# Forgetting attention with its scores made twice, in a hybrid trunk on one core

## The chip, the cores and the metric

The kernel runs on one core of a Trainium2 chip. The metric is the device time of one execution in microseconds. A core has five engines with queues of their own that work strictly in order: PE (matrix multiplication, with its weight loads PEld beside it), DVE (vector), ACT (scalar functions), POOL (the general vector engine) and SP, which here issues every DMA. Matmuls write PSUM, eight banks of 128 partitions by 512 floats; the other operands lie in SBUF. POOL reads and writes SBUF here, DVE and ACT both memories.

## The reference

One layer on x (2048 x 1024): h = RMSNorm(x); a projection of h to about 8,200 columns feeds three branches and a set of gates. The branches are forgetting attention (8 heads of 64), a gated delta rule (4 heads of 128 behind a causal convolution of four taps) and attention on a memory of 256 rows. Each branch is multiplied by a SiLU gate, projected to 1024 channels, weighted by a sigmoid gate and added; an output projection, the residual and a last RMSNorm follow. The part that matters here:

```python
s = jnp.einsum('bqhd,bkhd->bhqk', q_blk, k) * scale          # scale = 1/8
s = s + F_blk[..., :, None] - F[:, :, None, :]               # F: running sum of log-sigmoid
s = jnp.where(pos[None, None, None, :] <= p_blk[None, None, :, None], s, -jnp.inf)
p = jax.nn.softmax(s, axis=-1)
return jnp.einsum('bhqk,bkhd->bqhd', p.astype(v.dtype), v)   # then * silu(az)
```

All of it is float32. The kernel splits an operand into a high part of the matmul's rounded format (`F32R`) and a low part, the rest, and adds the products that matter.

## The kernel before, in words

A small planner (`Plan`) writes the program. Parts of the work are generators that say when their next step could start and how long it takes on PE; the planner keeps a clock for PE, ACT, DVE, POOL and the DMA queue, with costs by line, and always issues the first part that is ready, the dense matmuls last. The order that it finds is the order of the program on every engine; nothing is decided at run time.

The dense work, `dense()`, runs through the whole kernel: the input projection (tiles `pd_in`, 128 channels by 512 rows in 24 matmuls), then the branch projections (`branch`, tiles `pbr`, 12 matmuls each, for branch 1, branch 2, and the first two groups of 512 rows of branch 0, which is attention), then `branch_half` (tiles `pba`) for the other two groups, woven with the output projection (`pout`). The side work fills in: norm, logits, memory attention, the delta rule in three parts, and last `part_fox`, the forgetting attention. `part_fox` starts when the first half of the gate projections is done; from there the dense work beside it is the second half of the gate projections, then `pbr`. A `pbr` of branch 0 for a group of rows needs the attention output of all heads for that group (`load_ya`), so of the last head too.

In `part_fox` a unit is one head and 256 queries, 64 units in all, and three generators share the work. `prep` loads K and V of a head and splits them. `scores` makes, for each block of 128 queries, the scores with queries on the partitions: for each chunk of up to 512 keys two matmuls into a bank (L1084, L1087), the terms of F carried by four more rows of the operands, on the last chunk a third, of bfloat16, that adds the causal mask (L1086); DVE copies the bank to the tile `pr` and takes its maximum in the same instruction (L1088). `exps` gives ACT the exponential with the maximum as bias and the sum as a second output (L1106), and sends the reciprocals of the sums to DRAM. `values` transposes the probabilities on PE, four blocks of 128x128 to a bank (L1176, tile `ptp`); ACT rounds the bank to `ph` (L1181) and DVE subtracts, bank minus `ph`, to `plo` (L1182); two tiles later PE multiplies both with V (L1162, L1164, into `po`). `finish` loads the SiLU gate (`za`) and the reciprocals (`zl`), POOL multiplies the output with both, and SP stores it.

## Time and profile before

| what | number |
|---|---|
| median of 3 runs | 2749.91 us (2745.09 to 2751.78) |
| the profiled execution | 2749.7 us |
| its span, first to last instruction | 2747.7 us |
| mean granted clock of PE | 0.986 |
| PE, PEld | 96%, 80% of the span |
| DVE, ACT, POOL | 47%, 43%, 24% |
| bytes read and written | 213.75 and 133.40 MB |

A row of a group of instructions gives the line, the engine, the operation, what it writes and reads with the shapes and the count, then busy time and the mean time of one in ns, then the idle time of the engine before them and what ended it. Rows of a tile give count, shortest, median and longest time in ns, and the first and last start in us. Rows in order of time give the start and the time of one in us. Matmuls overlap, so their own times add up to more than PE's; the distance from one start to the next is what one costs.

### The profile page before, as it was taken

To read this page: it belongs to the slowest core of one execution; us is meant where nothing else is said; L and a number is where in the kernel's file an instruction comes from. 1 tells how busy PE (TensorE), PEld (TensorE's weight loads), DVE (VectorE), ACT (ScalarE), POOL (GpSimd) and SP (SyncE) were. 2 spreads that over 40 slices of the span, in tenths; PEclk is the share of its full clock that TensorE was granted. 3 is DMA by queue.
4 is the path that set the end of the run, shared out by engine and by line. 5 is a ranking of instruction groups with operands and counts; after the bars stand their busy time and mean duration, and the time that the engine had idled before them with its cause. 6 is when DMAs were issued, how large, how long until landed. Compare 5 with 4: busy or idle time off the path is not lost. (4 is left out here: it accounts for less than half of the span.)

```text
span 2747.7 us, 39152 instructions
## 1 busy us (share of the span) xinstructions
PE 2644.6 (96%) x13896; PEld 2196.4 (80%) x13896; DVE 1295.6 (47%) x3119; ACT 1182.4 (43%) x2469; POOL 657.5 (24%) x551
## 2 busy tenths in 40 slices
PE   7999999999999999899999999999999989988998
PEld 6778888888888888688788778788888778767887
DVE  6442656665333338122221356556556756334444
ACT  5531224342674421144334475666666645112221
POOL 0101110011333321222221432333333311453200
PEclk9999999999999999999999999999999999999999
DMA  5122222222656542455453332322222554888433
GB/s 184 51 79 84 85 84 66 70 85 77 202 184 205 187 147 85 135 161 157 151 159 121 102 81 65 78 69 76 85 75 60 136 144 117 295 279 287 152 122 108
DMA packets 256115, 349.74 MB, mean 127 GB/s; under 512 B 57808, under 2 KB 152272, under 8 KB 255648
## 3 DMA queue, kind: packets, MB, share of 16 engines
q1 hardware_dynamic: 255920, 347.25, 40.7%
q8 instruction: 109, 1.79, 0.3%
q14 instruction: 86, 0.70, 0.1%
HBM read 213.75 MB, written 133.40 MB: 126 GB/s over the span
## 5 line engine op out<-in xcount | busy, mean ns | idle before, releaser
L362 PE MATMUL pd_in<-hh,wh_in 128*128 128x512 f32 x1984 | 803.9, 405 | 8.5 <-ACT evg L399 8.5
L364 PE MATMUL pd_in<-hh,wl_in 128*128 128x512 f32 x1984 | 784.4, 395 | 3.5 <-POOL wl_in L346 2.4
L363 PE MATMUL pd_in<-hl,wh_in 128*128 128x512 f32 x1984 | 784.2, 395 | 0.0
L364 PEld LDWEIGHTS pd_in<-hh,wl_in 128*128 128x128 f32 x1984 | 374.4, 189 | 92.8 <-POOL wl_in L346 7.7
L362 PEld LDWEIGHTS pd_in<-hh,wh_in 128*128 128x128 f32 x1984 | 375.4, 189 | 83.6 <-ACT evg L399 8.9
L363 PEld LDWEIGHTS pd_in<-hl,wh_in 128*128 128x128 f32 x1984 | 375.4, 189 | 73.4
L346 POOL TENSOR_TENSOR wl_in<-wr_in,wh_in 128x1024 fp32r<-128x1024 f32 x88 | 214.6, 2440 | 908.9 <-ACT wh_in L342 860.2
L1182 DVE TENSOR_TENSOR plo<-ptp,ph 128x512 fp32r<-128x512 f32 (+1 forms) x288 | 178.6, 656 | 107.5 <-ACT ph L1181 106.5
L1106 ACT ACTIVATE pr<-pr,mx 128x1024 f32<-128x1024 f32 (+2 forms) x192 | 172.9, 902 | 93.6 <-DVE mx L1096 93.0
L1088 DVE TENSOR_SCALAR_CACHE_REDUCE pr<-pss 128x512 f32<-128x512 f32 (+2 forms) x320 | 185.7, 602 | 51.7 <-PE pss L1087 50.2
L1181 ACT CAST ph<-ptp 128x512 fp32r<-128x512 f32 (+1 forms) x288 | 149.6, 566 | 62.4 <-PE ptp L1176 61.1
L1162 PE MATMUL po<-ph,Vs 128*128 128x256 f32 x576 | 148.3, 294 | 17.7 <-ACT ph L1181 17.7
L342 ACT CAST wh_in<-wr_in 128x1024 fp32r<-128x1024 f32 x88 | 92.2, 1048 | 155.3 <-PE pd_in L363 147.5
L1176 PE MATMUL ptp<-ident,pr 128*128 128x128 f32 x1088 | 150.8, 274 | 4.2 <-ACT pr L1106 4.2
L1361 PE MATMUL pbr<-yh,wbh 128*128 128x512 f32 x320 | 129.1, 403 | 18.8 <-DVE gt L1386 9.9
L1176 PEld LDWEIGHTS ptp<-ident,pr 128*128 128x128 f32 x1088 | 126.4, 141 | 13.2 <-ACT pr L1106 4.9
L1164 PE MATMUL po<-plo,Vs 128*128 128x256 f32 (+1 forms) x512 | 133.4, 289 | 3.0 <-DVE plo L1182 2.5
L1162 PEld LDWEIGHTS po<-ph,Vs 128*128 128x128 f32 x576 | 110.2, 192 | 29.4 <-ACT ph L1181 21.2
L1362 PE MATMUL pbr<-yl,wbh 128*128 128x512 f32 x320 | 127.3, 398 | 1.9 <-DVE yl L558 1.9
L1363 PE MATMUL pbr<-yh,wbl 128*128 128x512 f32 x320 | 126.5, 395 | 0.0
L1087 PE MATMUL pss<-K,Q 128*128 128x512 f32 (+2 forms) x320 | 125.8, 396 | 0.5 <-POOL K L1008 0.5
L1084 PE MATMUL pss<-K,Q 128*128 128x512 f32 (+2 forms) x320 | 122.0, 382 | 1.5 <-DVE pr L1088 1.3
(324 smaller groups left out, 4410.6 us busy)
## 6 DMA issues: line engine op xcount, KB each, us to landing
wr_in<-in_w_in SPq DMA_DIRECT2D x88, 512.0 KB
dgt<-evg SPq DMA_DIRECT2D x96, 256.0 KB
gt<-dgt SPq DMA_DIRECT2D x96, 256.0 KB
dpt<-gt SPq DMA_DIRECT2D x80, 256.0 KB
pp<-dpt SPq DMA_DIRECT2D x64, 256.0 KB
dgq<-evv SPq DMA_DIRECT2D x48, 256.0 KB
kqv<-dgq SPq DMA_DIRECT2D x16, 768.0 KB
xt<-in_x SPq DMA_DIRECT2D x16, 512.0 KB
```

The source lines that it names most:

```text
L346: nc.gpsimd.tensor_sub(lo, raw, hi.bitcast(F32))
L362: nc.tensor.matmul(ps, wh[:, k, :], xh[:, k, :], start=(k == 0), stop=False)
L363: nc.tensor.matmul(ps, wh[:, k, :], xl[:, k, :], start=False, stop=False)
L364: nc.tensor.matmul(ps, wl[:, k, :], xh[:, k, :], start=False, stop=(k == kt - 1))
L1088: nc.vector.tensor_scalar(pr[:, ks], ps[:, 0:w], 1.0, None, ALU.mult, ALU.max, accum_out=nmx[:, j, ck:ck + 1])
L1106: nc.scalar.activation(pr[:, es], pr[:, es], AF.Exp, bias=mx[:, j:j + 1], scale=0.125, accum_out=lsp[:, j, e:e + 1])
L1162: nc.tensor.matmul(dst, Vk, ph[:, src], start=(v == 0 and b == 0), stop=False)
L1164: nc.tensor.matmul(dst, Vk, plo[:, src], start=False, stop=False)
L1176: nc.tensor.transpose(pt[:, o0:o0 + P], prs[j][0][:, (2 * v + b) * P:(2 * v + b + 1) * P], ident)
L1181: nc.scalar.copy(ph[:, 0:w], pt[:, 0:w])
L1182: nc.vector.tensor_sub(plo[:, 0:w], pt[:, 0:w], ph[:, 0:w].bitcast(F32))
L1361: nc.tensor.matmul(ps, wh[:, k, :], yh, start=(k == 0), stop=False)
```

## The change

Attention now works on units of one head and 512 queries, 32 in all. The scores are made twice.

`maxima` makes them with queries on the partitions, from the high parts alone (one matmul over 68 rows, tile `psm`), and only takes their maxima: DVE reduces each bank, the diagonal block after a mask add. The four maxima per partition are split in a high and a low part, transposed by one matmul (`ptm`) and written into eight more rows of the query operand `QA`, one pair for each block of 128 queries, so that the second scores come out with the maximum subtracted.

`values` makes the scores again with keys on the partitions (two matmuls, tile `pst`, up to 512 queries each), so that no transposes are needed: the mask is added by DVE in PSUM on diagonal blocks, ACT takes the exponential into `p` in SBUF, ACT rounds `p` to `ph`, DVE subtracts `p` minus `ph` to `plo`, and PE multiplies both with V over 512 queries. The sums over keys now run across partitions: POOL adds each `p` to a running tile `acc`, and `sums` splits it on DVE, sums it over the partitions with a matrix of ones on PE (`pL`), sends the row through DRAM to come back as 128x4, takes reciprocals there, and sends these through DRAM for the product. The bank rings are now two for maxima, two for scores, one for outputs and one for everything else.

The buffer of the convolution's input grows from 515 to 544 columns; the columns that are used stay the same.

```diff
-    dL = [dram.tile([256], F32, name=f"dL{n}") for n in range(8 * (S // 256))]
+    dL = [dram.tile([512], F32, name=f"dL{n}") for n in range(8 * NG)]
+    dR = [dram.tile([512], F32, name=f"dR{n}") for n in range(8 * NG)]
...
-            xb = hpA.tile([P, 515], F32, tag="xb", name="xb", bufs=2)
+            xb = hpA.tile([P, 544], F32, tag="xb", name="xb", bufs=2)
...
-        rs, rp, ro = Ring(psx, "s", 2), Ring(psx, "p", 3), Ring(psx, "o", 1)
+        rs, rp, ro, rm = Ring(psx, "s", 2), Ring(psx, "p", 2), Ring(psx, "o", 1), Ring(psx, "m", 1)
...
+                for ck in range(G + 1):
+                    for j in range(4):
+                        ks = slice(ck * 512, ck * 512 + (512 if ck < G else (j + 1) * P))
                         w = ks.stop - ks.start
...
-                        nc.tensor.matmul(ps[:, 0:w], Q1h[:, qs], K1h[:, ks], start=True, stop=False)
-                        if ck == nck - 1:
-                            nc.tensor.matmul(ps[:, w - P:w], identb, mneg, start=False, stop=False)
-                        nc.tensor.matmul(ps[:, 0:w], Q2h[:, qs], K2h[:, ks], start=False, stop=True)
-                        nc.vector.tensor_scalar(pr[:, ks], ps[:, 0:w], 1.0, None, ALU.mult, ALU.max,
-                                                accum_out=nmx[:, j, ck:ck + 1])
...
+                        nc.tensor.matmul(ps[:, 0:w], QAn[0:68, j * P:(j + 1) * P], KAh[0:68, ks], start=True, stop=True)
+                        e = pl.pe + pl.LAT
+                        if ck == G:
+                            nc.vector.tensor_tensor(dg[:, j, :], ps[:, w - P:w], mneg, ALU.add)
+                            e = pl.dve(P, e)
+                            w -= P
+                        if w:
+                            nc.vector.tensor_reduce(nmx[:, j, ck:ck + 1], ps[:, 0:w], AX.X, ALU.max)
...
+                nc.tensor.transpose(pt[0:104, 0:P], mt.bitcast(F32), ident)
+                nc.vector.tensor_tensor(QAn[96:104].rearrange("p (j n) -> p j n", j=4),
+                                        pt[96:104, 0:P].unsqueeze(1).to_broadcast([8, 4, P]), blk[96:104], ALU.mult)
...
+        def sums(n, oT, acc, ta):
...
+            nc.vector.tensor_copy(ah, acc)
+            nc.vector.tensor_sub(al, acc, ah.bitcast(F32))
...
+            nc.tensor.matmul(pL, ones, ah, start=True, stop=False)
+            nc.tensor.matmul(pL, ones, al, start=False, stop=True)
...
+            nc.scalar.copy(Ls, pL[0:1])
...
+            t1 = move(dL[n], Ls, 2)
...
+            t1 = move(lr, dL[n].rearrange("(p j) -> p j", j=4), 2)
...
+            nc.vector.reciprocal(rl, lr)
...
+            t1 = move(dR[n].rearrange("(p j) -> p j", j=4), rl, 2)
...
-                                nc.tensor.transpose(pt[:, o0:o0 + P],
-                                                    prs[j][0][:, (2 * v + b) * P:(2 * v + b + 1) * P], ident)
...
-                        nc.scalar.copy(ph[:, 0:w], pt[:, 0:w])
-                        nc.vector.tensor_sub(plo[:, 0:w], pt[:, 0:w], ph[:, 0:w].bitcast(F32))
...
+                        nc.tensor.matmul(ps[:, 0:w], KAh[:, ks], QAn[:, c0:512], start=True, stop=False)
+                        nc.tensor.matmul(ps[:, 0:w], KBh[:, ks], QBn[:, c0:512], start=False, stop=True)
+                        p = fx.tile([P, 512], F32, tag="p", name="p", bufs=3)
+                        t1 = pl.pe + pl.LAT
+                        if t >= 4 * G:
+                            nc.vector.tensor_tensor(ps[:, 0:P], ps[:, 0:P], mnegT, ALU.add)
+                            t1 = pl.dve(P, t1)
+                        nc.scalar.activation(p[:, 0:w], ps[:, 0:w], AF.Exp, scale=0.125)
...
+                        nc.scalar.copy(ph[:, 0:w], p[:, 0:w])
+                        t2 = pl.act(w, t1)
+                        nc.vector.tensor_sub(plo[:, 0:w], p[:, 0:w], ph[:, 0:w].bitcast(F32))
+                        t2 = pl.dve(w, t2)
+                        if t:
+                            nc.gpsimd.tensor_add(acc[:, c0:512], acc[:, c0:512], p[:, 0:w])
+                            ta = pl.pool(w, max(ta, t1))
```

The change also moves work on every engine. The first place is PE where attention ends. Before, the last value matmuls (`po`) are followed by branch projections (`pbr`) of branch 2, group 2:

```order
L1162 MATMUL po<-ph,Vs 128x128
L1164 MATMUL po<-plo,Vs 128x128
L1192 MATMUL po<-plo,Vs 128x256
L1361 MATMUL pbr_2_21930<-yh,wbh_20358 128x512
L1362 MATMUL pbr_2_21930<-yl,wbh_20358 128x512
L1363 MATMUL pbr_2_21930<-yh,wbl_20360 128x512
```

In the changed kernel the last projection of branch 2 (group 3) stands ten units of attention before the end:

```order
L1389 MATMUL pbr_3_19679<-yh,wbh_18095 128x512
L1390 MATMUL pbr_3_19679<-yl,wbh_18095 128x512
L1391 MATMUL pbr_3_19679<-yh,wbl_18097 128x512
L1216 MATMUL po<-ph,Vs 128x512
L1218 MATMUL po<-plo,Vs 128x512
L1183 MATMUL pst<-QA_12109,KA_12105 128x256
L1184 MATMUL pst<-QB_12111,KB_12107 128x256
```

and its last value matmuls stand among the projections of branch 0, with the first `pba` 24 `pbr` and two `pL` matmuls behind them:

```order
L1216 MATMUL po<-ph,Vs 128x128
L1218 MATMUL po<-plo,Vs 128x128
L1219 MATMUL po<-plo,Vs 128x512
L1389 MATMUL pbr_1_22378<-yh,wbh_19903 128x512
L1390 MATMUL pbr_1_22378<-yl,wbh_19903 128x512
L1391 MATMUL pbr_1_22378<-yh,wbl_19905 128x512
```

So the branch projections that stood behind attention now stand beside it, and in between lie eight units with hardly any of them.

The second place is POOL in the second half of attention. Before, it splits queries and weights and multiplies outputs:

```order
L346 TENSOR_TENSOR wl_in_2_17117<-wr_in_2_17028,wh_in_2_17115 128x1024
L1130 TENSOR_TENSOR oT<-oT,za 64x256
L1053 TENSOR_TENSOR Q_1_12116<-qr,Q_1_12116 64x256
L1131 TENSOR_TENSOR oT<-oT,zl 64x256
L1130 TENSOR_TENSOR oT<-oT,za 64x256
```

In the changed kernel, in a unit without filler:

```order
L1200 TENSOR_TENSOR acc<-acc,p 128x512 x8
L1200 TENSOR_TENSOR acc<-acc,p 128x384
L1200 TENSOR_TENSOR acc<-acc,p 128x256
L1061 TENSOR_TENSOR QB_12110<-qr,QA_12108 64x512
L1200 TENSOR_TENSOR acc<-acc,p 128x128
L1152 TENSOR_TENSOR oT<-oT,zl 64x512
L1151 TENSOR_TENSOR oT<-oT,za 64x512
```

An addition to `acc` for each tile of probabilities has come in, between the products with loaded tiles that were there.

The third place is DVE, at the end of a unit. Before, it copies scores, takes maxima and subtracts from PSUM (`ptp`):

```order
L1182 TENSOR_TENSOR plo<-ptp,ph 128x512 x2
L1182 TENSOR_TENSOR plo<-ptp,ph 128x384
L1088 TENSOR_SCALAR pr,nmx<-pss 128x512 x2
L1095 TENSOR_REDUCE mx<-nmx 128x1
L1096 TENSOR_SCALAR mx<-mx 128x1
```

In the changed kernel:

```order
L1197 TENSOR_TENSOR plo<-p,ph 128x384
L1188 TENSOR_TENSOR pst<-pst,mnegT 128x128
L1197 TENSOR_TENSOR plo<-p,ph 128x256
L1087 TENSOR_TENSOR dg<-psm,mneg 128x128 x2
L1119 CAST ah<-acc 128x512
L1197 TENSOR_TENSOR plo<-p,ph 128x128
L1120 TENSOR_TENSOR al<-acc,ah 128x512
```

The subtraction now reads `p` from SBUF, and the mask adds and the split of the sum have come in between.

More of the change, by code (lines that the diff above doesn't have):

```diff
@@ L959, in part_fox @@
         psx = fs.enter_context(tc.tile_pool(name="psx", bufs=2, space=PSUM))
-        rs, rp, ro = Ring(psx, "s", 2), Ring(psx, "p", 3), Ring(psx, "o", 1)
+        rs, rp, ro, rm = Ring(psx, "s", 2), Ring(psx, "p", 2), Ring(psx, "o", 1), Ring(psx, "m", 1)
         LAG = 2
-        XW = 1024
         fx = fs.enter_context(tc.tile_pool(name="fx", bufs=1))
-        mneg = fx.tile([P, P], BF16, name="mneg")
-        identb = fx.tile([P, P], BF16, name="identb")
+        KA = [fx.tile([P, S], F32R, name=f"KA{i}") for i in range(2)]
@@ L966, in part_fox @@
+        KB = [fx.tile([P, S], F32R, name=f"KB{i}") for i in range(2)]
+        QA = [fx.tile([P, 512], F32R, name=f"QA{i}") for i in range(2)]
+        QB = [fx.tile([P, 512], F32R, name=f"QB{i}") for i in range(2)]
+        blk = fx.tile([P, 4, P], F32, name="blk")
+        ones = fx.tile([P, P], F32R, name="ones")
+        mneg = fx.tile([P, P], F32, name="mneg")
         nc.gpsimd.memset(mneg, 0.0)
         nc.gpsimd.affine_select(mneg, mneg, [[-1, P]], ALU.is_ge, -1e30, base=0, channel_multiplier=1)
-        nc.vector.tensor_copy(identb, ident)
@@ new lines, in part_fox @@
+            eng.memset(KA[i][96:104].bitcast(F32), -1.0)
+        nc.vector.memset(ones.bitcast(F32), 1.0)
+        nc.gpsimd.memset(blk, 1.0)
+        nc.gpsimd.affine_select(blk, blk, [[-2, 4], [0, P]], ALU.is_ge, 0.0, base=-96, channel_multiplier=1)
+        nc.gpsimd.affine_select(blk, blk, [[2, 4], [0, P]], ALU.is_ge, 0.0, base=97, channel_multiplier=-1)
+        mts = [fx.tile([P, 104], F32R, name=f"mt{i}") for i in range(2)]
+        for i in range(2):
+            nc.vector.memset(mts[i].bitcast(F32), 0.0)
@@ L1017, in prep @@
                         nxt = raw(dv[g + 1], "vr")
-                    yield later(t0, rs.when), 0.44
-                    pt, kb = rs.take("ptv")
+                    yield later(t0, rm.when), 0.44
+                    pt, kb = rm.take("ptv")
                     pt = four(pt)
@@ L1195, in values @@
                 nc.scalar.activation(oT, po[64:128], AF.Copy, scale=0.5)
                 nc.vector.scalar_tensor_tensor(oT, po[0:64], 0.5, oT, ALU.mult, ALU.add)
-                ro.done(ko, pl.dve(256, pl.act(256, pl.pe + pl.LAT)))
-                finish(n, oT, r, hp, g, us)
+                ro.done(ko, pl.dve(512, pl.act(512, pl.pe + pl.LAT)))
                 st["pv"] = n + 1
+                pl.add(sums(n, oT, acc, ta))
+        OB = 3
         pl.add(values())
-        pl.add(scores())
+        pl.add(maxima())
```

275 lines of the change are left out of this document (128 added, 147 removed).

## Prediction

> **What bounds the kernel now.** I read the page's busy row first, then where the attention stage begins and ends, then its windows.
>
> ```profile
> span 2747.7 us, 39152 instructions
> PE 2644.6 (96%) x13896; PEld 2196.4 (80%) x13896; DVE 1295.6 (47%) x3119; ACT 1182.4 (43%) x2469; POOL 657.5 (24%) x551
> L1084 PE MATMUL pss<-K,Q x320: 218/393/628, 1537.8 to 2308.1; 128*128 128x512 f32 x128, 128*128 128x128 f32 x16, 128*128 128x384 f32 x16
> L1162 PE MATMUL po<-ph,Vs x576: 220/280/583, 1556.4 to 2327.1; 128*128 128x256 f32 x192
> L1487 PE MATMUL pba<-yh,wbh x128: 277/283/415, 2509.3 to 2608.8; 128*128 128x256 f32 x128
> 1537.80:2330.00 792.20, 763.33 (x4556) 647.95 (x4556) 474.30 (x1515) 502.10 (x1050) 246.30 (x254) 0.98 0.34 89
> 2330.00:2509.30 179.30, 158.84 (x668) 126.25 (x667) 58.36 (x80) 26.60 (x42) 79.71 (x63) 0.97 0.86 284
> ```
>
> PE is 96% busy, so PE sets the time. The window rows give length, then busy PE, PEld, DVE, ACT, POOL, the granted clock, the DMA share and GB/s. Attention runs from 1537.8 (first `pss`) to about 2327 (last `po`), woven with dense matmuls; after it PE still has 179 us of branch projections (`pbr`) before the first `pba` at 2509.3. Everything that the change touches lies between 1537.8 and 2509.3, 971.5 us, and the rest to the end is 2747.7 - 2509.3 = 238.4 us. Inside, DVE is busy 474 of 792 us and POOL 246: both have room today.
>
> A busy time of PE counts overlapping matmuls, so I price PE by start-to-start times:
>
> ```profile
> 2100.10 0.28 PE L1162 MATMUL po<-ph,Vs 128*128 128x256 f32 x1
> 2100.22 0.28 PE L1164 MATMUL po<-plo,Vs 128*128 128x256 f32 x1
> 2101.01 0.40 PE L1087 MATMUL pss<-K,Q 128*128 128x512 f32 x1
> 2101.24 0.40 PE L1084 MATMUL pss<-K,Q 128*128 128x512 f32 x1
> 2101.48 0.23 PE L1086 MATMUL pss<-mneg,identb 128*128 128x128 bf16 x1
> 2101.51 0.48 PE L1087 MATMUL pss<-K,Q 128*128 128x512 f32 x1
> 2101.83 0.28 PE L1162 MATMUL po<-ph,Vs 128*128 128x256 f32 x1
> 2110.49 1.47 PE L1176 MATMUL ptp<-ident,pr 128*128 128x128 f32 x12
> 2111.71 0.48 PE L362 MATMUL pd_in<-hh,wh_in 128*128 128x512 f32 x1
> ```
>
> So 512 columns cost 0.23 us, 256 cost 0.12, a transpose 1.22/12 = 0.10, a mask matmul 0.12 (0.03 until the next starts, which then takes 0.32, not 0.23). For 384 columns I put 0.175, between the two.
>
> **The change, part by part, on PE.** Removed: 1088 transposes (111 us at 1.22/12), 128 masks (15), 640 score matmuls (448 of 512 columns, 64 each of 384, 256 and 128: 103 + 25 = 128), and the value matmuls, 1024 of 256 and 128 of 128 columns (136): 390 us. Added: 320 score matmuls for the maxima (224 of 512, 32 each of 384, 256, 128: 51.5 + 12.6 = 64), 640 transposed score matmuls (128), 640 value matmuls over 512 queries (128), 64 of 512 against a matrix of ones for the sums (15), 32 transposes of the maxima (3): 338-339 us. The 128 transposes of V (11) stay. **PE saves 51 us.** If PE stayed the bound throughout, that would be the gain.
>
> The instruction order speaks against that. The dense filler beside attention is 1126 `pd_in` and 960 `pbr` matmuls before (259 + 221 = 480 us); the changed order issues 35 of the first before attention starts, which then starts 8 us later, at 1546. In 1546 to the first `pba` it has three parts:
> - A: 22 of the 32 attention units (212 of 320 key tiles), with 1091 `pd_in` and 768 `pbr`. PE: 212/320 of 350 us = 232, plus 251 and 177, 660 us.
> - B: 8 units (80 tiles) with only 18 `pbr`: 87 + 4 = 91 us of PE. No filler is left; the first group of branch 0, which comes next, needs the last head.
> - C: the last two units (28 tiles) with 174 `pbr`: 31 + 40 = 71 us.
>
> Before, all this filler outlasted attention; now attention outlasts it, and part B goes at the pace of the slowest other engine.
>
> **The pace of attention without filler.** Durations:
>
> ```profile
> L1182 DVE TENSOR_TENSOR plo<-ptp,ph 128x512 fp32r<-128x512 f32 x224 | 145.4, 686 | 99.2 <-ACT ph L1181 98.3
> L1182 DVE TENSOR_TENSOR plo<-ptp,ph 128x384 fp32r<-128x384 f32 x64 | 35.3, 552 | 8.3 <-ACT ph L1181 8.2
> L1196 DVE SCALAR_TENSOR_TENSOR oT<-po,oT 64x256 f32<-64x256 f32 x64 | 26.6, 416 | 46.2 <-ACT oT L1195 43.3 <-DMA dL<-rl 2.1 <-DMA qr<-dq 0.2
> L1390 POOL TENSOR_TENSOR gt<-gt,pp 128x512 f32<-128x512 f32 x46 | 59.3, 1297 | 62.9 <-DVE gt L1386 51.9 <-DMA pp<-dpt 10.8
> L1008 POOL TENSOR_TENSOR K<-kr,K 64x512 fp32r<-64x512 f32 x32 | 40.8, 1280 | 58.3 <-ACT K L1004 54.3 <-DMA zl<-dL 3.9
> L1053 POOL TENSOR_TENSOR Q<-qr,Q 64x256 fp32r<-64x256 f32 x62 | 45.6, 736 | 196.6 <-ACT Q L1046 145.8 <-issue 25.8 <-DMA wr_in<-in_w_in 10.0
> L399 ACT ACTIVATE evg<-pd_in,bmg 128x512 f32<-128x512 f32 x48 | 33.0, 688 | 14.6 <-PE pd_in L364 13.9 <-ACT K L1006 0.2
> L557 ACT CAST yh<-yr 128x512 fp32r<-128x512 f32 x42 | 25.8, 620 | 107.1 <-DMA yr<-dym 54.5 <-DMA yr<-dya 22.2 <-DMA yr<-dyb 17.2
> ```
>
> One head has 40 tiles: 28 of 512 queries, 4 each of 384, 256, 128.
> - POOL (its old work was light; the running sum `acc` is new): 24 adds of 512 at 1.30, 12 narrow ones at 1.02, 0.74, 0.45 (by line between 1297 and 736) = 40; K, Q and the two products on the output, 16 of 64x512 at 1.28 = 20. 60 us.
> - DVE: 28 `plo` at 0.69 and 12 narrow (0.55, 0.42, 0.28) = 24; 24 maxima over 512 at 0.69 and 12 narrow = 22 (no such reduction is in the rows; the nearest row of 512 from PSUM is 686); 32 mask adds of 128 at 0.28 = 9; copies and splits of the sum 7; some 2.8 per unit for small steps = 11; V 2. 74 us.
> - ACT: exp 28 at 0.69, cast 28 at 0.62, narrow ones 10, K and Q copies 10, output and sums 6: 63 us.
> - PE: 44 us.
>
> By busy time alone DVE sets 74 us a head, 148 us in B (two heads' worth of tiles). That is the floor of B; the other end comes from what DVE and POOL do to each other.
>
> ```profile
> L1182 DVE TENSOR_TENSOR plo<-ptp,ph x288: 536/681/693, 1551.9 to 2325.2; 128x512 fp32r<-128x512 f32 x112, 128x384 fp32r<-128x384 f32 x32
> L558 DVE TENSOR_TENSOR yl<-yr,yh x48: 676/691/1594, 2167.8 to 2537.8; 128x512 fp32r<-128x512 f32 x48
> L418 DVE TENSOR_SCALAR evv<-xb,cw x48: 486/489/2248, 264.7 to 694.3; 128x512 f32<-128x512 f32 x48
> 2362.63 1.29 POOL L1390 TENSOR_TENSOR gt<-gt,pp 128x512 f32<-128x512 f32 x1 [3.02 <-DVE gt L1386]
> 2362.87 1.59 DVE L558 TENSOR_TENSOR yl<-yr,yh 128x512 fp32r<-128x512 f32 x1 [0.32 <-ACT yh L557]
> 281.57 2.40 POOL L346 TENSOR_TENSOR wl_in<-wr_in,wh_in 128x1024 fp32r<-128x1024 f32 x1 [22.95 <-ACT wh_in L342]
> 282.01 2.25 DVE L418 TENSOR_SCALAR evv<-xb,cw 128x512 f32<-128x512 f32 x1 [3.17 <-ACT xb L415]
> ```
>
> The three numbers are min, median, max in ns. `plo` today subtracts an SBUF tile from a PSUM tile, and never takes over 693 ns. `yl` is the same subtraction with both inputs in SBUF: 0.69 us alone, up to 1.59; the one at 2362.87 ends 0.54 us after the POOL add that was running, as if it had waited for it. So does the single-source `evv` at 282.01. **The new `plo` has both inputs in SBUF (`p`, `ph`), and the new `acc` add runs on POOL once for nearly every tile.** If they take turns, a head needs POOL's 60 us plus DVE's own operations of this kind (24 `plo` and 7): 91 us, with the rest of DVE hidden under POOL's turns. B is then 183 us. I take this end, since the rows show it wherever the two meet.
>
> [...]
>
> C by the same turns: 28 tiles at 91/40 = 2.28 us is 64, plus 16 additions to `gt` at 1.30 (21) and 12 `yl` at 0.69 (8): 93 us, over PE's 71. A by the same turns: 212 x 2.28 = 483, 23 weight splits `wl_in` at 2.40 (55), 24 `wbl` of 128x512 (31), 32 `gt` (42), 32 `yl` (22): 633 us, under PE's 660. So A stays with PE, and I give it the loss that the stage has today: PE work before is 401 + 480 = 881 of 971.5 us, 10.3% over (waits, and a clock of 0.98). 660 x 1.103 = 728 us.
>
> The conv buffer (544 columns, not 515) changes no instruction's size: `evv` reads the same 512 columns. It costs nothing while PE is the bound there; at worst (the 144 + 48 conv instructions a tenth slower, uncovered) 14 us, at best a few us gained. The two loads and stores more per unit for the sums (a row out, back as 128x4, the reciprocal out) hang only on the output, three buffers deep, and SP issues fewer DMAs in all (8 for each of 32 units, before 6 for each of 64); uncovered only behind the last unit, where 24 `pbr` and 96 `pba` matmuls (5 + 12 us) stand ahead of the first that need it. I put 0, at worst 12 us.
>
> **Sum:** 1545.8 + 728 + 183 + 93 + 238.4 = 2788 us of span; the profiled execution took 2749.7 for a span of 2747.7, so 2 us lie around it: 2790 us. The profiled execution is within 0.2 us of the median of the three runs, 2749.91.
>
> **Rivals.**
> 1. *DVE and POOL hardly collide.* For: POOL's adds may fall into DVE's PSUM reads, whose durations never stretch. Against: `yl`. B takes DVE's 148, C PE's 71 x 1.103 = 78: 2738 span, 2740 us.
> 2. *PE's saving arrives.* DVE's small work overlaps better than in-order queues suggest, and B runs near PE's 91 x 1.1 = 100 with C 78: 2690 span, 2692 us. Against: 74 us of DVE work a head.
> 3. *The turns bite in A too.* [...] DVE also empties the score banks, two per ring; a late `plo` delays the next maximum, and then PE. POOL's products with the loaded reciprocals stand ahead of `acc` adds in its queue. If this doubles the loss in A, it adds 68 us, and the late output 12: 2868 span, 2870 us. It decides from the point where a wait of 1.3 us per tile no longer fits the two tiles between exp and value matmul.
>
> **How the numbers follow.** Forecast 0.52, rival 1 0.17, rival 2 0.07, rival 3 0.24. A change under 0.3% (8 us) can't be told from none here. The forecast's own range is 2755 to 2825 (A's loss between 7 and 14%, B between 170 and 195 us); all but its lowest edge is slower. Rival 1 at 2740 is at the edge of faster, so I split it: faster 0.09 + 0.07 = 0.16, the same 0.08 and 0.02 of the forecast = 0.10, slower 0.74. The range runs from below rival 1 to rival 3: 2725 to 2870. I predict **2790 us, 1.5% slower.**
>
> **What would show it.** In the changed profile: new `plo` with a mean clearly over 0.69 us and a maximum near 2 (right), or at 0.69 (rival 1); a stretch without `pd_in` and `pbr` of some 183 us in which PE is busy about half and POOL plus `plo` fill the time; PE's idle time put down to ACT and DVE tiles of attention, where before it had little; the last `po` within some 15 us of the first `pba`, not 182; the part before 1546 and the last 238 us unchanged. The prediction is wrong if that stretch is shorter than 150 us, or if A loses much more than a tenth.

## The result: 4.1% slower, and the profile after

| | before | changed |
|---|---|---|
| median | 2750.66 us (4 runs on the same chip) | 2861.10 us (4 runs, 2856.40 to 2867.26) |
| ratio | 1 | 1.0407, 95% interval 1.0382 to 1.0432 |
| profiled execution, its span | 2749.7, 2747.7 us | 2867.26, 2865.2 us |

The forecast was 2790 us, 1.5% slower, with a range of 2725 to 2870. The direction was right and the time lies in the range, but the loss is 110 us where 40 were forecast. First the head of the page of the changed kernel.

```profile
span 2865.2 us, 36512 instructions
...
PE 2686.9 (94%) x12584; PEld 2157.1 (75%) x12584; DVE 1618.1 (56%) x2896; ACT 1177.3 (41%) x2373; POOL 1036.0 (36%) x751
...
PE   7999999999999998999999999998988887788998
...
PEclk9999999999999999999999999999989976779999
```

PE is less busy than before (94% instead of 96%), DVE and POOL much more (DVE 1618 us instead of 1296, POOL 1036 instead of 658). In the last fifth of the span PE falls to 8 and 7 tenths, and the clock that was granted to it to 7 and 6. The rows of three tiles, and then the windows that they bound (columns as in the prediction: length, busy PE, PEld, DVE, ACT, POOL, clock, DMA share, GB/s), put that in its place:

```profile
L363 PE MATMUL pd_in<-hh,wh_in x1984: 387/390/796, 87.7 to 1922.4; 128*128 128x512 f32 x199
...
L1183 PE MATMUL pst<-QA,KA x320: 218/393/796, 1548.0 to 2613.2; 128*128 128x512 f32 x128, 128*128 128x256 f32 x32
...
L1514 PE MATMUL pba<-yh,wbh x128: 278/283/416, 2624.5 to 2726.4; 128*128 128x256 f32 x128
```

```profile
1541.20:2325.10 783.90, 726.60 (x3113) 565.50 (x3112) 593.52 (x961) 377.34 (x710) 492.62 (x357) 0.96 0.41 130
2325.10:2534.00 208.90, 164.45 (x458) 102.41 (x457) 183.36 (x307) 103.38 (x208) 130.52 (x100) 0.70 0.11 28
2534.00:2624.50 90.50, 77.49 (x308) 56.68 (x307) 77.79 (x103) 37.62 (x72) 66.71 (x46) 0.94 0.47 145
```

The windows are the prediction's A, B and C: from the start of attention to the end of the last filler matmul of branch 2 (2325.1), the stretch with next to no filler (to 2534.0), and the rest up to the first `pba`. In the second, DVE is busy 183 of 209 us, POOL 131, and PE's clock is 0.70 on the mean (0.50 from 2400 to 2420 us).

| part | forecast, us | measured, us | difference |
|---|---|---|---|
| up to the start of attention | 1545.8 | 1541.2 | -4.6 |
| A, with filler | 728 | 783.9 | +55.9 |
| B, without | 183 | 208.9 | +25.9 |
| C, up to the first `pba` | 93 | 90.5 | -2.5 |
| the rest | 238.4 | 240.7 | +2.3 |
| span | 2788.2 | 2865.2 | +77.0 |

So the miss lies in A and B. The groups by shape of the changed kernel show the operation that the prediction named, and beside it one that reads PSUM; the row of the tile has shortest, median and longest time, all widths together:

```profile
L1197 DVE TENSOR_TENSOR plo<-p,ph 128x512 fp32r<-128x512 f32 x224 | 297.9, 1358 | 34.0 <-ACT ph L1195 32.1 <-PE pL L1125 1.1 <-PE po L1218 0.3
L1200 POOL TENSOR_TENSOR acc<-acc,p 128x512 f32<-128x512 f32 x192 | 293.1, 1527 | 122.0 <-ACT p L1190 108.5 <-ACT ph L1195 3.2 <-DVE acc L1204 2.1
...
L1091 DVE TENSOR_REDUCE nmx<-psm 128x1 f32<-128x512 f32 x192 | 127.1, 680 | 18.2 <-PE psm L1084 17.2
```

```profile
L1197 DVE TENSOR_TENSOR plo<-p,ph x320: 274/1215/3029, 1550.8 to 2615.8; 128x512 fp32r<-128x512 f32 x128, 128x256 fp32r<-128x256 f32 x32
```

A subtraction `plo` of 512 columns takes 1.36 us on the mean and up to 3.03, where the same operation with one input in PSUM took 0.69. POOL's adds are stretched too: 1.53 us, where POOL operations of this form took 1.30 in the rows before. The maxima, which read PSUM, take 0.68 and never over 0.70. The order of time shows why, at two places of the changed kernel:

```profile
2331.11 1.27 POOL L1200 TENSOR_TENSOR acc<-acc,p 128x512 f32<-128x512 f32 x1 [0.71 <-ACT p L1190]
...
2331.57 1.36 DVE L1197 TENSOR_TENSOR plo<-p,ph 128x512 fp32r<-128x512 f32 x1 [0.28 <-ACT ph L1195]
...
2333.20 0.69 DVE L1197 TENSOR_TENSOR plo<-p,ph 128x512 fp32r<-128x512 f32 x1
```

```profile
2343.34 1.78 DVE L1197 TENSOR_TENSOR plo<-p,ph 128x512 fp32r<-128x512 f32 x1
2344.65 1.60 POOL L1200 TENSOR_TENSOR acc<-acc,p 128x512 f32<-128x512 f32 x1
...
2345.64 1.16 DVE L1197 TENSOR_TENSOR plo<-p,ph 128x512 fp32r<-128x512 f32 x1
```

The subtraction at 2331.57 starts inside an add that ends at 2332.38; it ends at 2332.93, 0.55 us after the add. The one at 2345.64 starts inside the add that ends at 2346.25 and ends at 2346.80, again 0.55 us after it. Over the whole trace, 28 subtractions of 512 columns start inside a POOL operation (over 10 ns after its start) and see no other one begin before their end: 26 of them end 547 to 554 ns after that operation. The other two start when less than 30 ns of it are left, and take their usual 0.68 us. The 36 that start outside any POOL operation, or within 10 ns of its start, all take under 0.70 us. The waits of the changed kernel between 1541 and 2625 us (total, times, longest) show who pays:

```profile
PEld po L1218 <- DVE plo L1197: 115.1, 121, 3.5
...
PE po L1218 <- DVE plo L1197: 69.0, 88, 3.0
...
PEld psm L1084 <- DVE nmx L1091: 17.3, 31, 1.4
...
PE psm L1084 <- DVE nmx L1091: 11.1, 20, 1.2
```

PE waits 69 us for `plo`, of the 115 us that it is idle in the three windows. The 115 us of the weight loads can't be added to that: 68.8 of the 69.0 us lie inside them. Before, in the same part of the kernel, PE waited 2.5 us for `plo`:

```profile
PE po L1164 <- DVE plo L1182: 2.5, 9, 0.3
```

### The profile page after: what moved, and what is told of

Read it like the earlier page. It is cut to its first block, busy times and chain, and to the rows that moved or that the text cites. A ratio compares the mean times of both kernels' runs of the same rounds, so it can differ in the third digit from the quotient of the medians.

```text
span 2865.2 us, 36512 instructions
## 1 busy us (share of the span) xinstructions
PE 2686.9 (94%) x12584; PEld 2157.1 (75%) x12584; DVE 1618.1 (56%) x2896; ACT 1177.3 (41%) x2373; POOL 1036.0 (36%) x751
## 4 chain that ended last, share of the span: by engine, by line
PE 31%; DVE 10%; DMA 4%; issue 4%; POOL 3%; ACT 2%; SPq 0%; DVEq 0%; POOLq 0%; ACTq 0%
DVE plo L1197 5%; PE pd_in L363 4%; PE pd_in L364 4%; PE pd_in L365 4%; PE pout L1544 2%; PE pout L1546 2%; PE pout L1545 2%; PE psm L1084 1%; PE pst L1183 1%; PE po L1218 1%; PE pst L1184 1%; POOL acc L1200 1%; DVE nmx L1091 1%; DMA dpt<-gt 1%; PE po L1216 1%
## 5 line engine op out<-in xcount | busy, mean ns | idle before, releaser
L363 PE MATMUL pd_in<-hh,wh_in 128*128 128x512 f32 x1984 | 798.5, 402 | 10.1 <-ACT evg L400 10.1
L365 PE MATMUL pd_in<-hh,wl_in 128*128 128x512 f32 x1984 | 780.5, 393 | 7.9 <-POOL wl_in L347 6.9
L364 PE MATMUL pd_in<-hl,wh_in 128*128 128x512 f32 x1984 | 779.4, 393 | 0.0
L365 PEld LDWEIGHTS pd_in<-hh,wl_in 128*128 128x128 f32 x1984 | 374.3, 189 | 92.2 <-POOL wl_in L347 12.6
L363 PEld LDWEIGHTS pd_in<-hh,wh_in 128*128 128x128 f32 x1984 | 375.3, 189 | 83.8 <-ACT evg L400 10.6
L1200 POOL TENSOR_TENSOR acc<-acc,p 128x512 f32<-128x512 f32 (+3 forms) x288 | 373.4, 1297 | 164.1 <-ACT p L1190 133.9
L364 PEld LDWEIGHTS pd_in<-hl,wh_in 128*128 128x128 f32 x1984 | 375.4, 189 | 70.1
L1197 DVE TENSOR_TENSOR plo<-p,ph 128x512 fp32r<-128x512 f32 (+1 forms) x320 | 382.5, 1220 | 67.2 <-ACT ph L1195 64.9
L1190 ACT ACTIVATE p<-pst 128x512 f32<-128x512 f32 (+1 forms) x320 | 167.5, 532 | 303.5 <-PE pst L1184 131.2
L1218 PE MATMUL po<-plo,Vs 128*128 128x512 f32 (+3 forms) x288 | 123.7, 430 | 69.9 <-DVE plo L1197 69.0
L1091 DVE TENSOR_REDUCE nmx<-psm 128x1 f32<-128x512 f32 (+3 forms) x288 | 166.7, 591 | 18.3 <-PE psm L1084 17.2
L1195 ACT CAST ph<-p 128x512 fp32r<-128x512 f32 (+1 forms) x320 | 171.0, 555 | 9.2 <-PE po L1216 3.4
L1084 PE MATMUL psm<-KA,QA 68*128 68x512 f32 (+2 forms) x320 | 130.7, 443 | 13.9 <-DVE nmx L1091 11.1
L1183 PE MATMUL pst<-QA,KA 128*128 128x512 f32 (+1 forms) x320 | 132.1, 413 | 8.9 <-DVE QA L1104 6.5
L1418 POOL TENSOR_TENSOR gt<-gt,pp 128x512 f32<-128x512 f32 x64 | 88.1, 1380 | 119.4 <-DVE gt L1414 82.5
L1184 PE MATMUL pst<-QB,KB 128*128 128x512 f32 (+1 forms) x320 | 129.3, 405 | 0.0
```

The lines of the kernel that those rows point to most:

```text
L363: nc.tensor.matmul(ps, wh[:, k, :], xh[:, k, :], start=(k == 0), stop=False)
L364: nc.tensor.matmul(ps, wh[:, k, :], xl[:, k, :], start=False, stop=False)
L365: nc.tensor.matmul(ps, wl[:, k, :], xh[:, k, :], start=False, stop=(k == kt - 1))
L1084: nc.tensor.matmul(ps[:, 0:w], QAn[0:68, j * P:(j + 1) * P], KAh[0:68, ks], start=True, stop=True)
L1091: nc.vector.tensor_reduce(nmx[:, j, ck:ck + 1], ps[:, 0:w], AX.X, ALU.max)
L1183: nc.tensor.matmul(ps[:, 0:w], KAh[:, ks], QAn[:, c0:512], start=True, stop=False)
```

## The experiments

Two questions were open: whether the turns of DVE and POOL are the whole loss, in A as well as in B, and by which way they cost what they do. "The region" is the time from the start of attention to the first `pba`: 971.5 us before, 1083.3 in the changed kernel.

### Without POOL's running sum

```diff
-                            nc.gpsimd.tensor_add(acc[:, c0:512], acc[:, c0:512], p[:, 0:w])
...
-                            nc.vector.tensor_copy(acc, p)
+                            nc.vector.tensor_scalar(acc, p, 1.0, None, ALU.add)
```

> The running sum is left out: POOL no longer adds each tile of probabilities to acc (the sums then hold only the first tile of keys plus one). PE, ACT and DVE work and their order stay. Turns theory (DVE's plo and POOL's add exclude each other): plo falls from a mean of 1.22 us to 0.69-0.8, the stretch without filler (2325 to 2534 in the changed kernel, 209 us) falls to DVE's own 148-165 us, part A (784 us) to 700-730, total 2740-2780 us. Clock or filler theory (the stretch is long because PE has no filler and its clock halves; POOL has no part in it): stretch about 200 us, total 2840-2865 us.

One run: 2761.46 us, beside 2751.98 for the kernel before. The windows of this kernel for A and B, and its `plo`:

```profile
1540.40:2275.50 735.10, 706.08 (x3112) 558.66 (x3111) 497.78 (x961) 377.56 (x710) 244.56 (x167) 0.98 0.45 138
2275.50:2440.30 164.80, 140.89 (x459) 90.15 (x457) 140.11 (x308) 100.74 (x208) 38.64 (x28) 0.77 0.14 36
```

```profile
L1197 DVE TENSOR_TENSOR plo<-p,ph 128x512 fp32r<-128x512 f32 x224 | 184.4, 847 | 58.3 <-ACT ph L1195 55.5 <-PE pst L1184 1.5
```

A falls from 784 to 735 us, B from 209 to 165, C from 90 to 80: the adds cost 104 us, 49 of them in A. What is left in A, 735 for the 660 of PE work, is 11% over, about the 10.3% that the prediction allowed. PE's waits for `plo` in A fall from 29.9 us to at most 11.9 (20.6 in the whole kernel without the adds, 8.7 of them in B). The 49 us have two halves: PE is idle for 28 us more with the adds (57 instead of 29), and busy 21 us longer with as many matmuls, at a granted clock of 0.96 instead of 0.98. In B it is some 20 and 24 us, at 0.70 instead of 0.77. `plo` still takes 0.85 us on the mean; POOL's older work is left. The window of B holds a second lesson: DVE is busy 140 of 165 us, so 25 us idle.

### Memsets in the place of the adds

```diff
-                            nc.gpsimd.tensor_add(acc[:, c0:512], acc[:, c0:512], p[:, 0:w])
+                            for _ in range(w // 128 + 1):
+                                nc.gpsimd.memset(junk, 0.0)
...
```

> In place of each add to acc POOL writes a small unused tile several times (w/128+1 memsets of 128x192, about 0.26 us each, so as long as the add), reading nothing; the running sum is left out. POOL is as busy as in the changed kernel. Turns theory, with the turns taken over SBUF reads: as without the adds, plo at 0.69-0.8 us, total 2740-2790 us. If POOL's occupied queue is the cause (outputs, K and Q splits come late behind the adds): as in the changed kernel, 2840-2865 us, though plo is at 0.69.

One run: 2881.64 us, but not as meant. The memsets wait for no data, so nearly all of them ran in the first 500 us of attention, where POOL's weight splits came late and A took 856 us; B and C had none and took 167 and 79, as without the adds. The time says nothing on the turns, then. The groups in 1540 to 2040 us do, first of this kernel, then of the one without add or memset:

```profile
L1202 POOL MEMSET junk<- 128x192 f32 x1242 | 325.1, 262 | 68.9
...
L1198 DVE TENSOR_TENSOR plo<-p,ph 128x512 fp32r<-128x512 f32 x71 | 63.2, 902 | 35.8 <-ACT ph L1196 35.5
```

```profile
L1197 DVE TENSOR_TENSOR plo<-p,ph 128x512 fp32r<-128x512 f32 x96 | 84.1, 890 | 36.9 <-ACT ph L1195 36.1
```

With 325 us of memsets beside it, `plo` takes 0.90 us; with none, 0.89. These operations of POOL, which only write, did not hold it up.

### The exponential left in PSUM

```diff
-                        p = fx.tile([P, 512], F32, tag="p", name="p", bufs=3)
+                        p = ps
...
-                        rp.done(kb, t1)
...
+                        rp.done(kb, t2)
...
-                            nc.gpsimd.tensor_add(acc[:, c0:512], acc[:, c0:512], p[:, 0:w])
+                            nc.gpsimd.tensor_add(acc[:, c0:512], acc[:, c0:512], ph[:, 0:w].bitcast(F32))
```

> The exponential is written back into its PSUM bank; ph is rounded from there, plo is bank minus ph, so one input of plo is in PSUM as before the change; POOL adds ph to acc (the low parts are left out of the sums). The bank is given back after plo, and the planner is told so. POOL adds as much as in the changed kernel. Turns theory: plo at 0.69 us, no wait for POOL; total 2730-2800 us although a bank is now held for some 2.5 us. If it is POOL's load or the lost filler alone: 2840-2900 us.

2831.12 us, ratio 1.0288 (1.0270 to 1.0305). Its `plo`, then A and B:

```profile
L1196 DVE TENSOR_TENSOR plo<-pst,ph x320: 275/681/694, 1547.8 to 2582.6; 128x512 fp32r<-128x512 f32 x128, 128x256 fp32r<-128x256 f32 x32
```

```profile
1538.20:2273.80 735.60, 694.74 (x3036) 550.00 (x3035) 433.73 (x894) 358.25 (x679) 428.95 (x341) 0.97 0.44 136
2273.80:2497.80 224.00, 188.27 (x526) 112.46 (x524) 163.17 (x373) 115.01 (x233) 130.38 (x114) 0.69 0.14 35
```

POOL adds as often and as much as in the changed kernel (the rounded part, so that the sums leave the low parts out), and `plo` never takes over 0.694 us, where it took up to 3.03 with both inputs in SBUF: with one input in PSUM, none of the 320 was stretched. The time missed both expectations, 2730 to 2800 us and 2840 or more. A is 735.6 us, as without the adds, but that is not like for like: the planner was told of the longer hold on the bank and made another order, in which A has 77 matmuls fewer (3036, not 3113) and B 68 more. The region is 1052.6 us, 31 less than in the changed kernel. B is longer, 224 us, with DVE busy only 163 of them. Each of the two banks of scores is held here through mask, exponential, rounding and subtraction, which may be a new wait in the place of the one removed. The runs further down with this edit come back to it.

### More matmuls in B

```diff
+                        for _ in range(3 if 22 <= n < 30 else 0):
+                            nc.tensor.matmul(ps[:, 0:w], KAh[:, ks], QAn[:, c0:512], start=True, stop=True)
```

> Three extra score matmuls (results overwritten) stand before each pst of units 22 to 29, the stretch without filler: 80 tiles x 3 x up to 0.23 us = 48 us more PE work there at full clock. Turns theory (PE is not the bound in that stretch): the granted clock there rises from 0.7 towards 1.0 and the stretch stays at 200-215 us, total 2850-2870 us. Clock theory (the half clock lengthens each tile's way): the stretch falls to 170-190 us, total 2825-2845 us. PE as bound: plus 40-90 us, 2900-2950 us.

One run: 2886.82 us. B of this kernel, to be set against B's row above:

```profile
2325.60:2546.60 221.00, 190.46 (x690) 131.39 (x689) 175.44 (x297) 110.19 (x208) 131.91 (x100) 0.82 0.11 27
```

The clock rose from 0.70 to 0.82 and B became 12 us longer, not shorter, a little more than the 200 to 215 us of the theory of turns. That speaks against a slow PE clock as what sets B, though not cleanly, since the 240 added matmuls are up to 48 us of PE work by themselves, and DVE is idle for 46 us here instead of 25. The next experiment has two kernels with the same clock in B.

### Half of each add

```diff
-                            nc.gpsimd.tensor_add(acc[:, c0:512], acc[:, c0:512], p[:, 0:w])
+                            nc.gpsimd.tensor_add(acc[:, c0:c0 + w // 2], acc[:, c0:c0 + w // 2], p[:, 0:w // 2])
...
```

> The changed kernel with POOL's running sum over half of the columns of each tile only (the other half of the sums is left out, and 1 is added to the first tile so that no sum is zero). Same number of POOL instructions, half their length. Theory (the price is the time for which POOL's add and DVE's subtraction keep each other out): about half of what leaving the add out altogether gave back, from 784 to 735 us in the filled part and from 209 to 165 in the bare one; so 760 and 187, and 2811 us in all, the mean of the subtraction of 512 columns near 1.0 us instead of 1.34. Rival (each add costs a fixed wait by its place in POOL's queue): 2845 us or more. Rival (only adds that are longer than the subtraction hurt): 2765 us, as without the add.

2791.74 us, ratio 1.0131 (1.0110 to 1.0152). A and B, and the two operations:

```profile
1540.40:2287.50 747.10, 710.57 (x3113) 557.25 (x3112) 529.85 (x961) 376.91 (x710) 394.67 (x357) 0.98 0.45 136
2287.50:2466.70 179.20, 147.48 (x459) 90.86 (x458) 154.23 (x308) 102.35 (x208) 95.18 (x100) 0.77 0.13 33
```

```profile
L1197 DVE TENSOR_TENSOR plo<-p,ph 128x512 fp32r<-128x512 f32 x224 | 219.8, 1006 | 45.3 <-ACT ph L1195 44.5
...
L1200 POOL TENSOR_TENSOR acc<-acc,p 128x256 f32<-128x256 f32 x192 | 179.5, 935 | 143.8 <-ACT p L1190 134.1 <-DVE acc L1204 1.7 <-ACT ph L1195 0.9
```

As many adds of half the width give back 37 of the 49 us in A and 30 of the 44 in B, three quarters and two thirds where half was expected; `plo` comes down to 1.01 us, as expected. The time, 2792 us, lies between the 2811 of the theory and the 2765 of the rival by which only adds longer than a subtraction hurt, so that rival may hold a part. It is mostly the length of the adds that costs, not their number. With half adds and with none, B's clock is the same 0.77, and yet B differs by 14 us, as DVE's busy time does. B's rows of three kernels now stand in one line: DVE busy 183.4, 154.2 and 140.1 us with whole, half and no adds, the stretch 208.9, 179.2 and 164.8. DVE's idle time is 25 us in each of them. **In these three, B is DVE's busy time, the turns in it included, plus 25 us.** In the two runs that change more than the adds it is not: DVE is idle for 46 us with the added matmuls and for 61 with the bank held.

### The filler spread over all of attention

```diff
...
+    def pace(n):
+        return lambda g: 0.0 if state["tiles"] >= n else INF
...
-            yield from dense_jobs([in_job(40 + i, ev_gate(i), HB) for i in range(24)], rd)
+            yield from dense_jobs([in_job(40 + i, ev_gate(i), HB, ready=pace(7.3 * i)) for i in range(24)], rd)
...
-                yield later(there(W[n, d]), ring.when), 0.0
+                yield later(there(W[n, d]), ring.when, lambda: pace(174 + 1.84 * (32 * n - 32 + 8 * g + d) if n else 0)(g)), 0.0
```

> The changed kernel with the dense matmuls beside attention handed out in step with the attention tiles, so that they last to its end and no stretch is without them; every instruction is the same, only the order differs. Theory (the loss is that attention without filler runs at the pace of DVE and POOL): with filler everywhere PE's work of attention and filler, some 822 us, comes near to setting the pace again, at a loss of 11 to 19 per cent as measured in the filled part: a region of 912 to 978 us instead of 1083, 2690 to 2760 us in all. Rival (turns between DVE and POOL set the pace everywhere, filled or not): their sum of some 910 us of the region is unchanged and each stretch of attention goes on at its pace of 2.6 us a tile in the end, region above 1040 us, 2820 us or more.

2851.14 us, ratio 1.0343 (1.0317 to 1.0369). The whole region of this kernel, and its waits for `plo`:

```profile
1541.30:2607.20 1065.90, 932.68 (x3876) 695.51 (x3875) 866.95 (x1369) 513.06 (x989) 692.76 (x503) 0.95 0.38 113
```

```profile
PEld po L1219 <- DVE plo L1197: 144.7, 134, 6.0
...
PE po L1219 <- DVE plo L1197: 92.5, 89, 5.8
```

The theory of the missing filler falls. No stretch of more than 21 us is bare any more and the clock is back at 0.95, yet the region is 1066 us, only 17 less than in the changed kernel; the rival's bound was 1040. PE now waits 93 us for `plo`, instead of 69, with filler queued behind each wait. (The 237 us in the next expectation is the sum of the two rows; it counts those waits twice.) So the filler's absence in B can't be the whole loss. It does cost something, but the turns hide it: without the adds, a run further down shows, spreading the filler is worth 57 us (980 to 923). The subtraction of this kernel:

```profile
L1197 DVE TENSOR_TENSOR plo<-p,ph 128x512 fp32r<-128x512 f32 x224 | 313.3, 1433 | 30.6 <-ACT ph L1195 30.1
```

### One tile more of slack

```diff
-        LAG = 2
+        LAG = 3
```

(on the spread kernel; the loads of gate and reciprocals are single in this one, to make room)

> The kernel with the dense matmuls spread over all of attention, and one thing more: the value matmuls come three tiles behind the scores and not two (the tiles of the two parts get a fourth buffer; the loads of gate and reciprocals are single, to make room). In the spread kernel PE's matmuls and weight loads wait 237 us for the subtraction of DVE, with all the filler queued behind them, in a region of 1066 us. Theory (lateness: the turns make a subtraction late for the value matmul, and what is queued behind it waits, while neither engine is short of time): one tile more, some 3.3 us, covers most of these waits; the region falls to 930 to 980 us, 2715 to 2765 us in all. Rival (rate: DVE and POOL together, one or the other busy for 93 per cent of the region, have no more to give): region above 1030 us, 2815 us or more, and the waits only move.

2843.48 us, ratio 1.0322 (1.0308 to 1.0336):

```profile
1539.40:2600.10 1060.70, 927.96 (x3877) 692.96 (x3876) 871.47 (x1367) 512.77 (x989) 699.42 (x502) 0.95 0.37 113
```

```profile
PEld po L1219 <- DVE plo L1197: 142.3, 141, 7.2
...
PE po L1219 <- DVE plo L1197: 90.7, 95, 7.1
```

The region is 1061 us and PE's waits for `plo` are 91: more slack gained 5 us, where 85 or more were expected. That leaves rate, in this order; `p` kept its three buffers, though, so the slack was not freed of every limit. The prediction's rival 3 described its step as a late `plo` that no longer fits two tiles; a third tile should have mended that, and here it didn't (in the changed kernel's own order it wasn't tried).

### Spread, with the exponential left in PSUM, and with more slack

The spreading and the edit that leaves the exponential in PSUM, together, then with `LAG = 3` as well.

> The same spreading of the dense matmuls, and the exponential left in PSUM so that the subtraction has one input there (no turns with POOL's adds; POOL adds the rounded part, so the sums leave the low parts out). Theory: both losses are gone, the region is PE's 822 us with the 10 to 12 per cent of loss that the run without turns had where it was filled, 905 to 920 us; 2685 to 2705 us in all, faster than the kernel before. Rival (the bank that is held until the subtraction is done limits the scores, ring of two): no better than the spreading alone, 2740 us or more.

> The spread kernel with the exponential left in PSUM and the subtraction from there (no turns; the sums leave the low parts out), and the value matmuls three tiles behind the scores. Without the third tile the region was 970 us for PE's 822. Theory (lateness again, now of the chain mask, exponential, rounding, subtraction): region 905 to 930 us, 2685 to 2710 us in all, clearly faster than the kernel before. Rival (each bank is held through that chain, and with two banks the scores come no sooner, however late the value matmuls are): no change beyond 10 us, 2740 to 2755 us.

2750.01 us, ratio 0.9991 (0.9977 to 1.0005), and 2749.14 us, 0.9985 (0.9974 to 0.9996): a tie with the kernel before, and a gain too small to count. The region of the first, and of the second:

```profile
1539.90:2510.30 970.40, 901.64 (x3877) 691.02 (x3875) 664.73 (x1371) 507.37 (x989) 620.22 (x503) 0.96 0.41 125
```

```profile
1540.70:2511.70 971.00, 902.48 (x3877) 689.73 (x3875) 666.24 (x1370) 506.86 (x989) 623.78 (x503) 0.96 0.42 125
```

With the adds still on POOL, but no turns between them and `plo`, the spread kernel's region is 970 us instead of 1066, so the loss is not POOL's load as such. Slack changes nothing. The 970 us are more than the 905 to 920 expected: PE's 822 us and 18% more. That the two banks, held longer, take the rest is what the rival said and fits, but a third bank wasn't tried, since all eight are in use.

### Spread, without the add, and with the add on DVE

```diff
-                            nc.gpsimd.tensor_add(acc[:, c0:512], acc[:, c0:512], p[:, 0:w])
+                            nc.vector.tensor_add(acc[:, c0:512], acc[:, c0:512], p[:, 0:w])
...
```

(the second, in which the planner also counts the adds on DVE and so makes a somewhat different order; the first leaves the line out; both on the spread kernel)

> The spread kernel without POOL's running sum (the sums over the keys are left out, 1 is added to the first tile). Same instructions otherwise. Theory (in the spread kernel DVE and POOL, taking turns, set the rate of the whole region): without the add no turns but those with POOL's older work, and the region falls from 1066 us by more than the 93 us that the bare order gave back, to 900 to 930 us; 2680 to 2715 us. Rival (something else keeps the spread order slow, such as the two banks of scores, the chain mask, exponential, rounding): 960 us or more, 2740 us or more, as with the exponential left in PSUM.

> The spread kernel with the running sum on DVE, not on POOL; nothing is left out. DVE gets 288 adds more, 0.69 us for 512 columns, some 24 us a head, 190 us in the region. Theory (the turns cost more than the add itself): DVE's own work is 98 us a head, 785 us plus its work for the filler, below the region's length, so the region falls below the 1066 us of the spread kernel although the busier engine has the work: 960 to 1010 us, 2740 to 2790 us. Rival (DVE's queue is full as it is): 1060 us or more, 2845 us or more.

2703.83 us, ratio 0.9821 (0.9803 to 0.9839), and 2784.29 us, 1.0113 (1.0092 to 1.0134). The regions:

```profile
1541.30:2464.10 922.80, 879.01 (x3877) 678.37 (x3876) 691.91 (x1369) 505.89 (x989) 311.70 (x215) 0.98 0.43 131
```

```profile
1539.10:2537.70 998.60, 912.45 (x3876) 686.58 (x3875) 875.72 (x1657) 507.54 (x989) 333.96 (x215) 0.96 0.40 121
```

Without the adds the region is 923 us, within the 900 to 930 expected; the adds on POOL cost 143 us of the spread kernel. On DVE, the busier engine, the same adds cost 76. The rows of the second:

```profile
L1197 DVE TENSOR_TENSOR plo<-p,ph 128x512 fp32r<-128x512 f32 x224 | 178.3, 812 | 5.7 <-ACT ph L1195 5.2
L1200 DVE TENSOR_TENSOR acc<-acc,p 128x512 f32<-128x512 f32 x192 | 153.8, 801 | 7.3 <-ACT p L1190 5.1
```

DVE is busy 876 us here and 867 in the spread kernel with the adds on POOL: it does 288 operations more in almost the same busy time, mainly because its subtractions take 0.81 instead of 1.43 us. POOL's help took about as much of DVE's time as the work itself would have.

### The conv buffer alone

```diff
-            xb = hpA.tile([P, 544], F32, tag="xb", name="xb", bufs=2)
+            xb = hpA.tile([P, 515], F32, tag="xb", name="xb", bufs=2)
```

(in the changed kernel; then 544 and 528 columns in the kernel before)

> The changed kernel with only the conv buffer back at 515 columns. My step that the buffer costs nothing: the time of the change, 2861 us, within 6 us, and attention starts at 1541 us within 3. Rival, the buffer is worth something by itself: at worst 14 us (the conv instructions a tenth slower), so 2847 or 2875 us, all of it ahead of 1541 us.

> The kernel before with only the conv buffer at 544 columns. Theory (the buffer's size moves the tiles of h that every dense matmul reads; the distance of two such matmuls was 230.7 ns with 515 columns and 227.4 with 544, and the changed kernel with 515 columns starts attention 11 us later): attention starts 11 us earlier, at 1527 us, more is gained beside attention, 2735 to 2742 us in all. My step that it costs nothing: 2750 us within 4.

> The kernel before with 528 columns in the conv buffer. In the compiled programs the tiles of h for rows 0 to 1023 begin 32 bytes past a multiple of 128 with 515 columns and 96 past one with 544 and with 528; against multiples of 256 they begin at 160, 224 and 96. Theory (what counts is the place within 128 bytes): matmuls 227.4 ns apart and 2740 us, as with 544. Rival (the place within 256 bytes or more): 230.7 ns and 2750 us or more, as with 515.

The changed kernel with 515 columns took 2879.86 us, ratio 1.0453 (1.0431 to 1.0475), and its attention starts at 1552.1 us, 10.9 later than with 544. The kernel before with 544 columns took 2740.25 us, ratio **0.9942 (0.9930 to 0.9955)**, with attention from 1523.9; with 528, 2752.23 us, ratio 0.9990 (0.9980 to 1.0000). So the step that the buffer costs nothing missed, and so did the guess that 544 columns gain more beside attention (in the kernel before with 544 the region is 975.7 us, 4 longer). Every instruction is the same in each pair. Windows of 800 to 1000 us, where PE never stops and about three quarters of its matmuls are dense ones: the changed kernel with 515 columns, with 544, the kernel before with 544, with 528.

```profile
800.00:1000.00 200.00, 200.00 (x937) 165.83 (x936) 66.27 (x177) 90.97 (x263) 76.78 (x68) 1.00 0.57 190
```

```profile
800.00:1000.00 200.00, 200.00 (x947) 167.96 (x946) 65.05 (x175) 87.15 (x260) 75.55 (x68) 1.00 0.58 196
```

```profile
800.00:1000.00 200.00, 200.00 (x948) 167.83 (x947) 64.92 (x175) 87.55 (x260) 74.52 (x68) 1.00 0.58 195
```

```profile
800.00:1000.00 200.00, 200.00 (x938) 166.35 (x937) 66.06 (x178) 92.34 (x264) 75.68 (x67) 1.00 0.58 193
```

In the same 200 us PE starts 937 matmuls with 515 columns, 947 and 948 with 544, 938 with 528; the clock is 1.00 in all of them. So PE gets 1.1% more matmuls done with 544; of the dense ones alone, the starts of two in a row are 227.3 ns apart in the changed kernel (L364 to L365), instead of 230.7 in the kernel before (L363 to L364), 1.5% less. The kernel before with 544 columns is the fastest kernel of this study that leaves nothing out, faster than both. The buffer's size moves the tiles of h that these matmuls read. By the addresses in the last expectation, their place within 128 bytes does not decide, since 528 has the same as 544 and the time of 515; what does was not settled, and other tiles behind the buffer were not looked at.

## Why the prediction was right and wrong, point by point

- **PE saves 51 us: it does, but doesn't arrive.** The spread kernel without the adds is 51 us faster than the kernel before; 14 of them are the buffer's, so by subtraction some 37 of PE's 51 arrive once the turns of `acc` are gone (in a kernel that leaves the sums out).
- **Attention starts 8 us later: the size was off in two directions.** With the buffer undone it starts 14.3 us later than before, with it 3.4. Two misses, this one and the buffer's, partly cancel here, by luck.
- **A, 660 us of PE and 10.3% more, 728: the term that failed most, by 56 us.** The step was "633 us, under PE's 660. So A stays with PE", and that a sum of turns just under PE's work costs nothing. It cost 49 us, shown by the run without the adds (735 us for as many matmuls): PE waits 29.9 us in A for a late `plo` instead of at most 11.9, and its matmuls are busy 21 us longer at a lower clock. Why the lateness arises although the sum lies under PE's work was not shown; as I read it, two in-order engines that wait for one another and stand near the pace of a third slow it too. The prediction named this as rival 3 with a price of 68 us and a chance of 0.24. Its reason, lateness against two tiles of slack, found no support in the spread order, where a third tile gained 5 us, and was not tested in A itself. The other 7 us are the allowance, 11.4% instead of 10.3.
- **B, 183 us: mis-sized by 26.** The mechanism was right in part: turns, not DVE's 148 us of busy time alone, and not PE's 100. But the step "with the rest of DVE hidden under POOL's turns" failed. Behind each of the 320 subtractions the next DVE operation starts 0.09 us before its end at the earliest: while a subtraction stands, the maxima behind it stand too. So the turns add to DVE's work and don't cover it: 140 us without adds, 43 more with them, 25 idle, 208 of the 209 measured. That POOL's and DVE's turns also came to 183 by my sum is a coincidence with DVE's busy time of 183.4, and an allowance for idle time, which A had, was missing in B.
- **C, the rest and the tail: right** within 2.5 us each, C's 93 us by the sum of turns; the late output cost nothing that can be seen.
- **The conv buffer, nothing: wrong.** It gained 0.6% alone, some 14 us; that the prediction gave the same size as its worst loss is chance. The step that failed was to price the instructions that use the buffer and none of those that read the tiles which it moves.
- **Rivals 1 and 2** needed a `plo` at 0.69 us; it took 1.36. By the prediction's own mark, that A loses much more than a tenth (it lost 18.8%), the forecast is wrong and rival 3 at 2870 us is nearer to the 2861 measured.

Who held up whom, as the runs show it: with one input in PSUM, no subtraction took over 0.694 us beside as many adds of POOL; with both in SBUF, the subtractions of 512 columns took 1.36 us on the mean beside the adds, and 0.90 beside memsets against 0.89 without. Of the 28 that started inside one POOL operation and met no other, 26 ended 0.55 us after it, less than the 0.69 that the subtraction takes alone. What that costs in time had to be read from the queue of the engine that waits.

## What to carry to other kernels

When an operation is moved to a second engine to unload a first, look at what the first does with the same memory: here the adds on POOL kept DVE standing, and in the spread kernel the same adds on DVE itself were 67 us cheaper. Price a wait on an in-order engine as added to all the work queued behind it: in B the adds made DVE busy for 43 us more, and the stretch 44 us longer. Leave an allowance of its own for a stage in which two other engines come near the bound: here 633 us of turns under 660 of PE cost 49 us beyond the usual tenth. Every size of a buffer is an edit of its own: time it alone, since here a few unused columns gave the only gain (0.6%) of the whole change.

## What the hardware showed that was not expected

- Dense matmuls of 512 columns started 230.7 ns apart on the mean in the kernel before (L363 to L364, 800 to 1000 us) and 227.3 in the changed kernel (L364 to L365), whose conv buffer has 544 columns, at a granted clock of 1.00 in both. With nothing changed but the size of that buffer, and so the place of what lies behind it, the kernel before started 936 matmuls in these 200 us with 515 columns, 938 with 528 and 948 with 544.
- A subtraction that was kept out by an add ended 0.55 us after it, where it takes 0.69 alone, as if some 0.14 us of it (an estimate, the difference of the two) went on while the add still ran.
- PE was granted 0.70 of its clock in a stretch of 209 us (B) in which it waited often but briefly, 1.5 us at the most and 44 us in all, and 0.82 with 240 more matmuls in it (221 us). What set the clock was not shown.
